# Merge stage by pairs of column chunks: another order of the branch products, and the gate tanh released earlier

## The chip, the cores and the metric

The kernel runs on one NeuronCore of one Trainium2 chip. The metric is the device time of one execution in microseconds. Before the change three runs took 836.33, 837.1 and 837.5 us, so the median is 837.1 us. The profile was taken from one more execution of 836.26 us.

## The reference, cut to what matters

One layer works on 512 tokens of width 1024. After an RMS norm, one projection makes the inputs of two branches, a matrix memory ("mLSTM", 4 heads of 128) and a differential attention (4 heads of 128), and two gates of width 1024. Each branch ends in a head norm. Then both branches go through a 512x1024 matrix of their own and are merged by the gates. An output projection, a gated feed-forward part, an embedding part and a last norm follow.

```
hm = head_rmsnorm(mlstm_chunkwise(...));  ya = (sigmoid(mo) * hm) @ w_br_m
hd = head_rmsnorm(diff_attention(...)) * (1 - lam_init);  yb = hd @ w_br_d
mixed = sigmoid(g_a) * ya + sigmoid(g_b) * yb
x = x + mixed @ w_out
```

## The kernel before

Activations lie with features on the 128 partitions and the 512 tokens along the free axis. So a vector of width 1024 is eight chunks of 128x512, and the result of one branch is four chunks, one per head (hm0 to hm3 of the memory, hd0 to hd3 of the attention). To keep precision every operand is split into a high and a low part (`split`, L86, recorded as L88 and L89, or L91 and L92 where there is a scale: ScalarE rounds to the high part, VectorE subtracts to get the low one). A product is then three matmuls, L96, L97 and L98 of `mm3`: high x high, low x high, high x low. In the products of the merge the weight is what the matmul calls whi and wlo.

Weights come by `wload` (L100): 512 KB from HBM into a buffer `raw`, then the split into `whi` and `wlo`. There are two buffers of each. The load and the split are given a raised priority, so they stand early in the order of their engines. A new `whi` can be written only when the last matmul that reads the old one in its buffer, an L97, has run.

The work of the two branches and of the first gates is written in the order of the table ORDER (L49). Its entries are steps such as `a3` (scores and probabilities of attention head 3), `A3` (the norm that ends that head) or `ga1` (a gate chunk), and a scheduler then sets the order of each engine at build time by priorities, data and free buffers. The last step is A3, that is `attention_end` (L491) for head 3: square (L405), a sum over the partitions on TensorE (`colsum`, tile hd3ss), VectorE L495, then `rsqrt_of` (L152: ScalarE Ln L157, Exp L159, Square L160, VectorE L161 and L162), VectorE L497 and the split that gives hdh and hdl of head 3.

The merge (L549 to L565) runs over eight column chunks j. For each it has two gate chunks (those for j = 0 to 3 come from the ORDER table, those for 4 to 7 are made in the loop), their tanh (L555, released by `issue_after` only when the last Exp of an `rsqrt_of` has been issued, which is that of head 3), one weight load that holds the 512 rows of the memory branch and the 512 of the attention branch for this column chunk, the products ya and yb of 12 matmuls each into two of the four PSUM buffers "mm", and on VectorE L560 to L562, which weight and add them, before the split into mxh and mxl. Two more PSUM buffers with the tag "acc" serve the two branches: num and den of the memory, av of the attention. ScalarE's activation functions come in table sets; a change of set is an instruction of its own, ACT_TABLE_LOAD.

Of the kernel before, what the change touches and what calls it, by code (L numbers as in the profile page):

```python
# [13 lines left out]
AF = mybir.ActivationFunctionType  # L14
ALU = mybir.AluOpType

P = 128
S = 512
D = 1024
KD = D // P  # L20
# [35 lines left out]
def trunk_kernel(ctx, tc, xT, pT, par, biasT, lamv, w_if, w_in, w_v, w_br, w_out, w_up,  # L56
                 w_down, w_gate, w_ple, gfin, out):
    nc = tc.nc
# [10 lines left out]
    def rt(tag, name):  # L69
        return big.tile([P, S], F32R, tag=tag, name=name, bufs=NBUF[tag])  # L70
# [5 lines left out]
    def ps(tag, name, n=S):  # L76
        return pp.tile([P, S], F32, tag=tag, name=name, bufs={"mm": 4, "sc": 2, "acc": 2}[tag])[:, :n]
# [8 lines left out]
    def split(hi, lo, src, scale=None):  # L86
        if scale is None:
            nc.scalar.copy(hi, src)  # L88
            nc.vector.tensor_sub(lo, src, f(hi))  # L89
        else:  # L90
            nc.scalar.activation(hi, src, AF.Copy, scale=scale)  # L91
            nc.vector.scalar_tensor_tensor(lo, src, scale, f(hi), op0=ALU.mult, op1=ALU.subtract)  # L92
# [7 lines left out]
    def wload(src, n=1024):  # L100
        raw = wp.tile([P, 1024], F32, tag="raw", name="raw", bufs=2)
        hi = wp.tile([P, 1024], F32R, tag="whi", name="whi", bufs=2)
        lo = wp.tile([P, 1024], F32R, tag="wlo", name="wlo", bufs=2)
        with tc.high_priority(offset=180):
            nc.sync.dma_start(raw[:, :n], src)
            split(hi[:, :n], lo[:, :n], raw[:, :n])
        return hi, lo
# [4 lines left out]
    def proj(o, w, k0, acts, start=True, stop=True):  # L112
        n = len(acts)
        for i, a in enumerate(acts):
            mm3(o, wk(w, k0 + i), a, start and i == 0, stop and i == n - 1)
# [14 lines left out]
    lnb = cp.tile([P, 1], F32, name="lnb")  # L130
# [16 lines left out]
            nc.scalar.activation(q, src, AF.Square)  # L147
            nc.vector.tensor_add(acc, acc, q)

    last_exp = None  # L150

    def rsqrt_of(r, v, a, before=None):  # L152

        if before is not None:
            with tc.issue_after(before.ins):
                nc.scalar.preload_act_table_set("natural_log_exp_and_others")
        nc.scalar.activation(r, v, AF.Ln, scale=2.0 ** -LN_SHIFT)  # L157
        nonlocal last_exp
        last_exp = nc.scalar.activation(r, r, AF.Exp, scale=-0.5, bias=lnb)  # L159
        nc.scalar.activation(a, r, AF.Square)  # L160
        nc.vector.scalar_tensor_tensor(a, v, -0.5, a, op0=ALU.mult, op1=ALU.mult)  # L161
        nc.vector.scalar_tensor_tensor(r, a, 1.5, r, op0=ALU.add, op1=ALU.mult)  # L162
# [19 lines left out]
    acc = tt("mo", "acc")  # L182
# [273 lines left out]
        return hi, lo  # L456


    def attention(hh, q, k):
        av = []  # L460
        for i in range(NB):
            n = (i + 1) * P
            nw = max(n, 2 * P)
            es, sums = [], []
            for z in range(2):
                s = ps("sc", f"ds{hh}{i}{z}", nw)
                for b in range(2):
                    nc.tensor.matmul(s, lhsT=q[z][:, i * P:(i + 1) * P], rhs=k[z][b][:, :nw],  # L468
                                     start=b == 0, stop=b == 1)
                e = tt("e" if z == 0 else "rb", f"e{z}", n)  # L470
                mx = tp.tile([P, 4], F32, tag="mx", name="mx", bufs=8)
                nc.vector.tensor_tensor_reduce(  # L472
                    out=e, in0=s[:, :n], in1=bias[hh][:, S - n:], scale=1.0, scalar=-3.0e38,
                    op0=ALU.add, op1=ALU.max, accum_out=mx[:, 0:1])
                nc.vector.tensor_scalar_mul(mx[:, 1:2], mx[:, 0:1], -1.0)  # L475
                nc.scalar.activation(e, e, AF.Exp, bias=mx[:, 1:2], accum_out=mx[:, 2:3])  # L476
                nc.vector.reciprocal(mx[:, 3:4], mx[:, 2:3])
                es.append(e)
                sums.append(mx[:, 3:4])
            nc.vector.tensor_scalar(es[1], es[1], sums[1], nlam, op0=ALU.mult, op1=ALU.mult)  # L480
            nc.vector.scalar_tensor_tensor(es[0], es[0], sums[0], es[1], op0=ALU.mult, op1=ALU.add)
            av.append(es[0])
        o = ps("acc", f"av{hh}")
        for j in range(NB):
            tps = ps("sc", f"at{hh}{j}", S - j * P)
            for i in range(j, NB):
                nc.tensor.transpose(tps[:, (i - j) * P:(i - j + 1) * P], av[i][:, j * P:(j + 1) * P], ident)
            weighted("a", j, lambda a, b: split(a, b, tps), dv, hh, (o,))
        return o
# [12 lines left out]
    def gate(c, name):  # L502
        o = ps("mm", name)
        proj(o, win(c), 0, h)
        t = tt("x", name)
        nc.vector.tensor_mul(t, o, rB)
        return t
# [3 lines left out]
    mq, mk, dq, dk, mo, sums, hm, hd, ga, gb = ({} for _ in range(10))  # L511
    for step in ORDER.split():
        what, i = step[:-1], int(step[-1])
# [18 lines left out]
        elif what == "bias":  # L532
            bias, nlam = make_bias(), make_nlam()
# [12 lines left out]
    hm, hd = ([t[i] for i in range(H)] for t in (hm, hd))  # L546


    mixed = []  # L549
    for j in range(KD):  # L550
        ta = ga[j] if j in ga else gate(20 + j, "ga")
        tb = gb[j] if j in gb else gate(28 + j, "gb")
        with tc.issue_after(last_exp.ins):
            for t in (ta, tb):
                nc.scalar.activation(t, t, AF.Tanh, scale=0.5)  # L555
        w = wload(w_br[j])
        oa, ob = ps("mm", "ya"), ps("mm", "yb")
        proj(oa, w, 0, hm)
        proj(ob, w, 4, hd)
        nc.vector.scalar_tensor_tensor(ta, ta, 1.0, oa, op0=ALU.add, op1=ALU.mult)  # L560
        nc.vector.scalar_tensor_tensor(tb, tb, 1.0, ob, op0=ALU.add, op1=ALU.mult)
        nc.vector.tensor_add(ta, ta, tb)  # L562
        hi, lo = rt("v", f"mxh{j}"), rt("v", f"mxl{j}")
        split(hi, lo, ta, 0.5)
        mixed.append((hi, lo))  # L565


    x2, h2 = [], []
    acc = tt("mo", "acc")
# [27 lines left out]
    for c in range(KF):  # L597
# [4 lines left out]
        hi, lo = rt(gtag[c], f"gh{c}"), rt(gtag[c], f"gl{c}")  # L602
# [10 lines left out]
    for k in range(2):  # L613
        t = tt("hn", "pt")
# [10 lines left out]
    for n in range(2):  # L625
        w = wload(w_ple[n])
# [10 lines left out]
    acc = tt("mo", "acc")  # L637
# [140 lines left out]
def _chunks(w):  # L778

    k, n = w.shape  # L780
    return w.reshape(k // P, P, n // P, P).transpose(2, 1, 0, 3).reshape(n // P, P, k)
# [25 lines left out]
def _pack(x, p, rel_bias, norm_mix_g, w_in, b_if, m_conv_w, m_conv_b, m_norm_g, da_lambda, da_norm_g,  # L807
          w_br_m, w_br_d, w_out, norm_ffn_g, w_up, ffn_conv_w, ffn_conv_b, w_down, norm_ple_g,
          w_ple_gate, w_ple, norm_final_g):
    w = w_in[0]  # L810
    mq, mk, mv, mo = (w[:, 512 * i:512 * (i + 1)] for i in range(4))
    gif = np.zeros((D, 64), np.float32)
    gif[:, 0:H] = w[:, 2048:2052]
    gif[:, 32:32 + H] = w[:, 2052:2056]
    dq, dk, dv = (w[:, 2056 + 512 * i:2056 + 512 * (i + 1)] for i in range(3))
    win = np.concatenate([mq, mk, dq, dk, mo, w[:, 3592:]], axis=1)
    wv = np.concatenate([v.reshape(4, 2, P, S).transpose(0, 2, 1, 3).reshape(4, P, 2 * S) for v in (mv, dv)])
    nf = DFF // P
    order = np.stack([nf + np.arange(nf), np.arange(nf)], axis=1).ravel()
    wup = _chunks(w_up[0])[order]  # L820
    par = np.zeros((P, NPAR), np.float32)
    for c, v in ((C_GMIX, norm_mix_g[0]), (C_GFFN, norm_ffn_g[0]), (C_GPLE, norm_ple_g[0]),
                 (C_GM, m_norm_g[0]), (C_GD, da_norm_g[0])):
        v = _cols(v)
        par[:, c:c + v.shape[1]] = v
    mc = np.concatenate([m_conv_w[0], m_conv_b], axis=0)
    par[:, C_MCONV:C_MCONV + 40] = mc.reshape(5, 8, P).transpose(2, 1, 0).reshape(P, 40)
    fc = np.concatenate([ffn_conv_w[0], ffn_conv_b], axis=0)
    par[:, C_FCONV:C_FCONV + 176] = fc.reshape(4, 2 * nf, P)[:, order].transpose(2, 1, 0).reshape(P, 176)
    par[0:H, C_B] = b_if[0, :H]  # L830
    par[32:32 + H, C_B] = b_if[0, H:]
    return {
        "xT": _fmajor(x[0]), "pT": _fmajor(p[0, 0]), "par": par, "biasT": _bias_tiles(rel_bias),
        "lamv": da_lambda[0],
        "w_if": gif.reshape(KD, P, 64).transpose(1, 0, 2).reshape(P, KD * 64), "w_in": _chunks(win), "w_v": wv,
        "w_br": np.concatenate([_chunks(w_br_m[0]), _chunks(w_br_d[0])], axis=2),
        "w_out": _chunks(w_out[0]), "w_up": wup, "w_down": _chunks(w_down[0]),
        "w_gate": w_ple_gate[0].reshape(KD, P, D), "w_ple": w_ple[0].reshape(2, P, 2, S).transpose(2, 1, 0, 3).reshape(2, P, D), "gfin": norm_final_g[None],
    }
# [18 lines left out]
```

## Time and profile before

| | |
|---|---|
| median of 3 runs | 837.1 us (836.33 to 837.5) |
| profiled execution | 836.26 us |
| its span, first to last instruction | 833.3 us |
| mean granted TensorE clock | 0.992 of full speed |
| TensorE matmuls | 811.2 us busy, 97% |
| VectorE / ScalarE | 539.7 us (65%) / 397.8 us (48%) |
| HBM | 101 GB/s over the span |

The page gives the busy time of each engine, the span in 40 slices with the granted clock, and the chain of work that ended last. A timeline row has the start in us, the duration, the engine, the line in the kernel, the operation, output and inputs by the program's names, shapes and a count; in brackets stands the idle time ahead of it and what ended it. A full-speed matmul of 512 columns is shown as 0.39 us long, but the next one starts 0.23 us later, because matmuls overlap.

### The profile page before, as it was taken

To read this page: it belongs to the slowest core of one execution; us is meant where nothing else is said; L and a number is where in the kernel's file an instruction comes from. 1 tells how busy PE (TensorE), PEld (TensorE's weight loads), DVE (VectorE), ACT (ScalarE), POOL (GpSimd) and SP (SyncE) were. 2 spreads that over 40 slices of the span, in tenths; PEclk is the share of its full clock that TensorE was granted. 3 is DMA by queue.
4 is the path that set the end of the run, shared out by engine and by line. 5 is a ranking of instruction groups with operands and counts; after the bars stand their busy time and mean duration, and the time that the engine had idled before them with its cause. 6 is when DMAs were issued, how large, how long until landed. Compare 5 with 4: busy or idle time off the path is not lost.

```text
span 833.3 us, 9859 instructions
## 1 busy us (share of the span) xinstructions
PE 811.2 (97%) x3661; PEld 665.4 (80%) x3661; DVE 539.7 (65%) x873; ACT 397.8 (48%) x614; POOL 27.3 (3%) x111
## 2 busy tenths in 40 slices
PE   8999999999999699999999999999999999999995
PEld 6878878878777588888788888888888888888884
DVE  7689885589977654455677777777777333343545
ACT  6546854487664632334554444444444432232434
POOL 0011200000000000000000000000000000000000
PEclk9999999999999899999999999999999999999998
DMA  6242532212222122252322222223223323333402
GB/s 245 77 131 98 174 115 74 101 51 76 77 77 76 51 101 101 96 187 97 126 102 94 87 97 101 101 102 115 89 99 102 95 89 96 95 112 96 147 31 76
DMA packets 28119, 84.54 MB, mean 101 GB/s; under 512 B 3316, under 2 KB 4992, under 8 KB 28072
## 3 DMA queue, kind: packets, MB, share of 16 engines
q1 hardware_dynamic: 27256, 81.96, 28.9%
q0 software_dynamic: 528, 1.70, 0.7%
q8 instruction: 28, 0.46, 0.2%
q10 hardware_dynamic: 288, 0.27, 0.1%
q14 instruction: 19, 0.16, 0.1%
HBM read 81.79 MB, written 2.13 MB: 101 GB/s over the span
## 4 chain that ended last, share of the span: by engine, by line
PE 81%; ACT 2%; issue 1%; DVE 1%; POOL 0%; POOLq 0%; DVEq 0%; ACTq 0%
PE uv L96 5%; PE wd L98 5%; PE wd L96 5%; PE uv L98 5%; PE uv L97 5%; PE wd L97 5%; PE ug L96 5%; PE ug L98 5%; PE ug L97 5%; PE ga L96 2%; PE ga L98 2%; PE ga L97 2%; PE gb L98 2%; PE gb L97 2%; PE gb L96 2%; PE wo L96 2%
## 5 line engine op out<-in xcount | busy, mean ns | idle before, releaser
L88 ACT CAST whi<-raw 128x1024 fp32r<-128x1024 f32 (+1 forms) x136 | 137.7, 1013 | 221.5 <-issue 72.5
L89 DVE TENSOR_TENSOR wlo<-raw,whi 128x1024 fp32r<-128x1024 f32 (+2 forms) x135 | 159.3, 1180 | 89.5 <-ACT whi L88 88.1
L97 PE MATMUL wd<-gl,whi 128*128 128x512 f32 x176 | 68.5, 389 | 0.0
L98 PE MATMUL wd<-gh,wlo 128*128 128x512 f32 x176 | 68.5, 389 | 0.0
L96 PE MATMUL wd<-gh,whi 128*128 128x512 f32 x176 | 68.5, 389 | 0.0
L592 DVE SCALAR_TENSOR_TENSOR y<-u,prm,y 128x512 f32<-128x512 f32 x88 | 65.6, 749 | 1.5
L88 ACT CAST gh<-y 128x512 fp32r<-128x512 f32 x22 | 13.7, 622 | 55.6 <-DVE y L601 55.6
L587 DVE TENSOR_TENSOR u<-uv,rffn 128x512 f32<-128x512 f32 x22 | 15.2, 692 | 38.1 <-PE uv L98 38.1
L97 PEld LDWEIGHTS wd<-gl,whi 128*128 128x128 f32 x176 | 33.0, 188 | 6.9
L98 PEld LDWEIGHTS wd<-gh,wlo 128*128 128x128 f32 x176 | 33.0, 188 | 6.9
L96 PEld LDWEIGHTS wd<-gh,whi 128*128 128x128 f32 x176 | 33.0, 188 | 6.8
L590 ACT ACTIVATE y<-u,prm 128x512 f32<-128x512 f32 x44 | 35.7, 812 | 0.5 <-DVE u L587 0.3
L599 ACT ACTIVATE y<-y 128x512 f32<-128x512 f32 x22 | 13.9, 632 | 38.7 <-DVE y L592 38.7
L96 PE MATMUL wo<-mxh,whi 128*128 128x512 f32 x64 | 24.9, 389 | 0.0
L97 PE MATMUL wo<-mxl,whi 128*128 128x512 f32 x64 | 24.9, 389 | 0.0
L98 PE MATMUL wo<-mxh,wlo 128*128 128x512 f32 x64 | 24.9, 389 | 0.0
L89 DVE TENSOR_TENSOR gl<-y,gh 128x512 fp32r<-128x512 f32 x22 | 15.2, 692 | 14.7 <-ACT gh L88 14.7
L476 ACT ACTIVATE e<-e,mx 128x128 f32<-128x128 f32 (+3 forms) x32 | 17.8, 556 | 7.8 <-DVE mx L475 7.8
L96 PE MATMUL yb<-hdh,whi 128*128 128x512 f32 x32 | 13.2, 412 | 6.5 <-ACT hdh L91 6.5
L224 DVE SCALAR_TENSOR_TENSOR y<-u,prm,y 128x512 f32<-128x512 f32 x24 | 17.9, 744 | 0.1
L472 DVE CUSTOM_DVE_ANT_0 e<-ds,bias 128x128 f32<-128x128 f32 (+3 forms) x32 | 15.3, 484 | 3.2 <-PE ds L468 3.0
L575 DVE TENSOR_TENSOR x<-x,wo 128x512 f32<-128x512 f32 x8 | 5.5, 688 | 17.2 <-PE wo L98 17.2
(1081 smaller groups left out, 2200.8 us busy)
## 6 DMA issues: line engine op xcount, KB each, us to landing
raw<-in_w_up SPq DMA_DIRECT2D x44, 512.0 KB, 3.2
raw<-in_w_in SPq DMA_DIRECT2D x36, 512.0 KB, 3.2
raw<-in_w_down SPq DMA_DIRECT2D x16, 512.0 KB, 3.5
x<-in_xT SPq DMA_DIRECT2D x16, 256.0 KB, 4.7
raw<-in_w_br SPq DMA_DIRECT2D x8, 512.0 KB, 3.1
raw<-in_w_out SPq DMA_DIRECT2D x8, 512.0 KB, 3.3
raw<-in_w_gate SPq DMA_DIRECT2D x8, 512.0 KB, 3.3
raw<-in_w_down SPq DMA_DIRECT2D x8, 384.0 KB, 3.1
```

The costliest lines, as they stand in the source:

```text
L88: nc.scalar.copy(hi, src)
L89: nc.vector.tensor_sub(lo, src, f(hi))
L96: nc.tensor.matmul(o, lhsT=lh, rhs=rh, start=start, stop=False)
L97: nc.tensor.matmul(o, lhsT=lh, rhs=rl, start=False, stop=False)
L98: nc.tensor.matmul(o, lhsT=ll, rhs=rh, start=False, stop=stop)
L224: nc.vector.scalar_tensor_tensor(y, u[:, i:i + S], col(c0 + i), y, op0=ALU.mult, op1=ALU.add)
L472: nc.vector.tensor_tensor_reduce(out=e, in0=s[:, :n], in1=bias[hh][:, S - n:], scale=1.0, scalar=-3.0e38, op0=ALU.add, op1=ALU.max, accum_ ...
L476: nc.scalar.activation(e, e, AF.Exp, bias=mx[:, 1:2], accum_out=mx[:, 2:3])
L587: nc.vector.tensor_mul(u[:, 2:514], o, rB)
L590: nc.scalar.activation(y, u[:, 2:514], AF.Identity, scale=col(c0 + 2), bias=col(c0 + 3))
L592: nc.vector.scalar_tensor_tensor(y, u[:, i:i + S], col(c0 + i), y, op0=ALU.mult, op1=ALU.add)
L599: nc.scalar.activation(gt, gt, AF.Gelu_apprx_tanh)
```

## The change

The merge loop now runs over pairs of column chunks (m = 0, 2, 4, 6). The weight array is laid out anew on the host: a load of 512 KB holds one branch for both chunks of the pair, the first the memory branch's, the second the attention branch's. So the order of the products in a pair is ya, ya, yb, yb, with a weight load ahead of each two. The two ya of the second pair (m = 2) take their PSUM from the tag "acc". The tanh of the gates is released by the last Exp of a softmax in `attention` in place of the last Exp of an `rsqrt_of`. The arithmetic is the same.

```diff
--- before.py
+++ after.py
@@ -147,16 +147,13 @@
             nc.scalar.activation(q, src, AF.Square)
             nc.vector.tensor_add(acc, acc, q)
 
-    last_exp = None
-
     def rsqrt_of(r, v, a, before=None):
 
         if before is not None:
             with tc.issue_after(before.ins):
                 nc.scalar.preload_act_table_set("natural_log_exp_and_others")
         nc.scalar.activation(r, v, AF.Ln, scale=2.0 ** -LN_SHIFT)
-        nonlocal last_exp
-        last_exp = nc.scalar.activation(r, r, AF.Exp, scale=-0.5, bias=lnb)
+        nc.scalar.activation(r, r, AF.Exp, scale=-0.5, bias=lnb)
         nc.scalar.activation(a, r, AF.Square)
         nc.vector.scalar_tensor_tensor(a, v, -0.5, a, op0=ALU.mult, op1=ALU.mult)
         nc.vector.scalar_tensor_tensor(r, a, 1.5, r, op0=ALU.add, op1=ALU.mult)
@@ -456,7 +453,10 @@
         return hi, lo
 
 
+    last_softmax = None
+
     def attention(hh, q, k):
+        nonlocal last_softmax
         av = []
         for i in range(NB):
             n = (i + 1) * P
@@ -473,7 +473,7 @@
                     out=e, in0=s[:, :n], in1=bias[hh][:, S - n:], scale=1.0, scalar=-3.0e38,
                     op0=ALU.add, op1=ALU.max, accum_out=mx[:, 0:1])
                 nc.vector.tensor_scalar_mul(mx[:, 1:2], mx[:, 0:1], -1.0)
-                nc.scalar.activation(e, e, AF.Exp, bias=mx[:, 1:2], accum_out=mx[:, 2:3])
+                last_softmax = nc.scalar.activation(e, e, AF.Exp, bias=mx[:, 1:2], accum_out=mx[:, 2:3])
                 nc.vector.reciprocal(mx[:, 3:4], mx[:, 2:3])
                 es.append(e)
                 sums.append(mx[:, 3:4])
@@ -546,23 +546,28 @@
     hm, hd = ([t[i] for i in range(H)] for t in (hm, hd))
 
 
+
     mixed = []
-    for j in range(KD):
-        ta = ga[j] if j in ga else gate(20 + j, "ga")
-        tb = gb[j] if j in gb else gate(28 + j, "gb")
-        with tc.issue_after(last_exp.ins):
-            for t in (ta, tb):
+    for m in range(0, KD, 2):
+        js = (m, m + 1)
+        gates = [(ga[j] if j in ga else gate(20 + j, "ga"), gb[j] if j in gb else gate(28 + j, "gb")) for j in js]
+        with tc.issue_after(last_softmax.ins):
+            for t in (t for pr in gates for t in pr):
                 nc.scalar.activation(t, t, AF.Tanh, scale=0.5)
-        w = wload(w_br[j])
-        oa, ob = ps("mm", "ya"), ps("mm", "yb")
-        proj(oa, w, 0, hm)
-        proj(ob, w, 4, hd)
-        nc.vector.scalar_tensor_tensor(ta, ta, 1.0, oa, op0=ALU.add, op1=ALU.mult)
-        nc.vector.scalar_tensor_tensor(tb, tb, 1.0, ob, op0=ALU.add, op1=ALU.mult)
-        nc.vector.tensor_add(ta, ta, tb)
-        hi, lo = rt("v", f"mxh{j}"), rt("v", f"mxl{j}")
-        split(hi, lo, ta, 0.5)
-        mixed.append((hi, lo))
+        outs = []
+        for n, (tag, ys) in enumerate((("acc" if m == 2 else "mm", hm), ("mm", hd))):
+            w = wload(w_br[m + n])
+            outs.append([ps(tag, ("ya", "yb")[n]) for _ in js])
+            for i in range(2):
+                proj(outs[n][i], w, 4 * i, ys)
+        for i, j in enumerate(js):
+            ta, tb = gates[i]
+            nc.vector.scalar_tensor_tensor(ta, ta, 1.0, outs[0][i], op0=ALU.add, op1=ALU.mult)
+            nc.vector.scalar_tensor_tensor(tb, tb, 1.0, outs[1][i], op0=ALU.add, op1=ALU.mult)
+            nc.vector.tensor_add(ta, ta, tb)
+            hi, lo = rt("v", f"mxh{j}"), rt("v", f"mxl{j}")
+            split(hi, lo, ta, 0.5)
+            mixed.append((hi, lo))
 
 
     x2, h2 = [], []
@@ -833,7 +838,8 @@
         "xT": _fmajor(x[0]), "pT": _fmajor(p[0, 0]), "par": par, "biasT": _bias_tiles(rel_bias),
         "lamv": da_lambda[0],
         "w_if": gif.reshape(KD, P, 64).transpose(1, 0, 2).reshape(P, KD * 64), "w_in": _chunks(win), "w_v": wv,
-        "w_br": np.concatenate([_chunks(w_br_m[0]), _chunks(w_br_d[0])], axis=2),
+        "w_br": np.stack([_chunks(v[0]).reshape(4, 2, P, S).transpose(0, 2, 1, 3).reshape(4, P, 2 * S)
+                          for v in (w_br_m, w_br_d)], axis=1).reshape(KD, P, 2 * S),
         "w_out": _chunks(w_out[0]), "w_up": wup, "w_down": _chunks(w_down[0]),
         "w_gate": w_ple_gate[0].reshape(KD, P, D), "w_ple": w_ple[0].reshape(2, P, 2, S).transpose(2, 1, 0, 3).reshape(2, P, D), "gfin": norm_final_g[None],
     }
```

The order on ScalarE, from the split of the weights loaded last before the attention's end (aph: high part of the turned probabilities of head 3; av3: its output; whi: weights; ga, gb: gates). Before:

```order
L88 CAST whi_2742<-raw_2741 128x1024
L88 CAST aph_2504<-at30_2499 128x512
L88 CAST aph_2515<-at31_2511 128x384
L88 CAST aph_2525<-at32_2522 128x256
L88 CAST aph_2534<-at33_2532 128x128
L493 ACTIVATE y_2675<-av3_2498,prm_72 128x512
L405 ACTIVATE v_2676<-av3_2498 128x512
L166 CAST csph_2681<-v_2676 128x512
L157 ACTIVATE r_2677<-v_2676 128x512
L159 ACTIVATE r_2677<-r_2677,lnb_91 128x512
L555 ACT_TABLE_LOAD
L555 ACTIVATE ga_2293<-ga_2293 128x512
```

In the changed program, from the same place:

```order
L88 CAST whi_2735<-raw_2734 128x1024
L556 ACT_TABLE_LOAD
L556 ACTIVATE ga_2293<-ga_2293 128x512
L556 ACTIVATE gb_2640<-gb_2640 128x512
L556 ACTIVATE gb_2359<-gb_2359 128x512
L88 CAST aph_2504<-at30_2499 128x512
L88 CAST aph_2515<-at31_2511 128x384
L556 ACTIVATE ga_2673<-ga_2673 128x512
L556 ACTIVATE ga_2326<-ga_2326 128x512
L556 ACTIVATE gb_2607<-gb_2607 128x512
L556 ACTIVATE ga_2061<-ga_2061 128x512
L88 CAST aph_2525<-at32_2522 128x256
```

and farther on, from the next weight split to the end of head 3 (hdh3):

```order
L402 ACTIVATE v_2676<-av3_2498 128x512
L163 CAST csph_2681<-v_2676 128x512
L155 ACT_TABLE_LOAD
L155 ACTIVATE r_2677<-v_2676 128x512
L156 ACT_TABLE_LOAD
L156 ACTIVATE r_2677<-r_2677,lnb_91 128x512
L157 ACTIVATE hd3ss_2680<-r_2677 128x512
L88 CAST whi_2817<-raw_2816 128x1024
L91 ACTIVATE hdh3_2694<-y_2675 128x512
```

One table load and seven tanh now stand ahead of or between the four casts aph, and an eighth behind them. Ln and Exp of head 3 have a table load each, and a weight cast (whi_2817) stands ahead of hdh3.

The order on TensorE at the last matmuls ahead of those that read hdh3 (yb_2707 and yb_2748 are yb of column chunks 0 and 1, ya_2788 is ya of chunk 2). Before:

```order
L98 MATMUL yb_2748<-hdh1_1930,wlo_2743 128x512
L96 MATMUL yb_2748<-hdh2_2258,whi_2742 128x512
L97 MATMUL yb_2748<-hdl2_2259,whi_2742 128x512
L98 MATMUL yb_2748<-hdh2_2258,wlo_2743 128x512
L96 MATMUL yb_2707<-hdh3_2694,whi_2701 128x512
L97 MATMUL yb_2707<-hdl3_2695,whi_2701 128x512
L98 MATMUL yb_2707<-hdh3_2694,wlo_2702 128x512
L96 MATMUL yb_2748<-hdh3_2694,whi_2742 128x512
L97 MATMUL yb_2748<-hdl3_2695,whi_2742 128x512
L98 MATMUL yb_2748<-hdh3_2694,wlo_2743 128x512
L96 MATMUL ya_2788<-hmh0_1907,whi_2783 128x512
```

In the changed program (yb_2740 and yb_2741 are yb of chunks 0 and 1, ya_2791 is ya of chunk 3, yb_2822 and yb_2823 are yb of chunks 2 and 3):

```order
L97 MATMUL ya_2791<-hml3_2415,whi_2785 128x512
L98 MATMUL ya_2791<-hmh3_2414,wlo_2786 128x512
L96 MATMUL yb_2822<-hdh0_1770,whi_2817 128x512
L97 MATMUL yb_2822<-hdl0_1771,whi_2817 128x512
L96 MATMUL yb_2823<-hdh0_1770,whi_2817 128x512
L96 MATMUL yb_2740<-hdh3_2694,whi_2735 128x512
L96 MATMUL yb_2741<-hdh3_2694,whi_2735 128x512
L97 MATMUL yb_2823<-hdl0_1771,whi_2817 128x512
L98 MATMUL yb_2822<-hdh0_1770,wlo_2818 128x512
L96 MATMUL yb_2822<-hdh1_1930,whi_2817 128x512
L97 MATMUL yb_2822<-hdl1_1931,whi_2817 128x512
L97 MATMUL yb_2740<-hdl3_2695,whi_2735 128x512
```

Between the last yb on hdh2 of chunk 1 and the first matmul on hdh3 stand now the 24 matmuls of ya of chunks 2 and 3 (ya_2790 and ya_2791, of which the piece shows the last two rows) and three matmuls on the weights whi_2817, which are split into the buffer that ya_2791's weights held.

## Rows read from the trace of the kernel before

**Rows 1.** The page, busy time, share of the span and instructions of each engine:
```profile
PE 811.2 (97%) x3661; PEld 665.4 (80%) x3661; DVE 539.7 (65%) x873; ACT 397.8 (48%) x614; POOL 27.3 (3%) x111
```

**Rows 2.** Waits of TensorE: us in total, times, longest:
```profile
PE yb L96 <- ACT hdh L91: 6.5, 1, 6.5
...
PE s L96 <- ACT mk0h L91: 1.4, 1, 1.4
```

**Rows 3.** Timeline of TensorE, from the wait to the gates behind the fourth chunk:
```profile
273.81 0.39 PE L98 MATMUL yb<-hdh,wlo 128*128 128x512 f32 x1
280.68 0.79 PE L96 MATMUL yb<-hdh,whi 128*128 128x512 f32 x1 [6.48 <-ACT hdh L91]
...
284.84 0.40 PE L98 MATMUL ya<-hmh,wlo 128*128 128x512 f32 x1
...
295.08 0.39 PE L96 MATMUL ga<-h0h,whi 128*128 128x512 f32 x1
...
300.07 0.39 PE L97 MATMUL ga<-h7l,whi 128*128 128x512 f32 x1
...
300.52 0.39 PE L96 MATMUL gb<-h0h,whi 128*128 128x512 f32 x1
```

**Rows 4.** Stretches: us, busy time by engine, granted clock (PEclk), DMA share, GB/s:
```profile
60.00:62.00 2.00, 0.66 (x3) 0.49 (x3) 1.30 (x2) 1.62 (x3) 1.02 (x3) 1.00 0.53 178
...
277.00:278.00 1.00, 0.00 (x0) 0.00 (x0) 0.97 (x3) 1.00 (x3) 0.00 (x0) 0.92 0.00 0
278.00:279.00 1.00, 0.00 (x0) 0.00 (x0) 1.00 (x2) 1.00 (x4) 0.00 (x0) 0.50 0.00 0
...
284.00:285.00 1.00, 1.00 (x4) 0.73 (x4) 1.00 (x2) 0.56 (x1) 0.00 (x0) 0.67 0.00 0
...
295.00:327.70 32.70, 32.70 (x146) 27.07 (x145) 15.28 (x18) 9.69 (x12) 0.00 (x0) 1.00 0.28 97
```

**Rows 5.** Timeline of ScalarE, from the last softmax on:
```profile
260.64 1.05 ACT L88 CAST whi<-raw 128x1024 fp32r<-128x1024 f32 x1
264.41 0.97 ACT L88 CAST aph<-at 128x512 fp32r<-128x512 f32 x2 [2.72 <-PE at L487]
267.37 0.54 ACT L88 CAST aph<-at 128x256 fp32r<-128x256 f32 x2 [1.99 <-PE at L487]
...
270.48 0.62 ACT L166 CAST csph<-v 128x512 fp32r<-128x512 f32 x1
273.14 0.63 ACT L157 ACTIVATE r<-v 128x512 f32<-128x512 f32 x1 [2.04 <-DVE v L495]
273.80 0.72 ACT L159 ACTIVATE r<-r,lnb 128x512 f32<-128x512 f32 x1
274.54 1.28 ACT L555 ACT_TABLE_LOAD   x1
275.84 0.63 ACT L555 ACTIVATE ga<-ga 128x512 f32<-128x512 f32 x1
...
280.01 0.61 ACT L91 ACTIVATE hdh<-y 128x512 fp32r<-128x512 f32 x1
...
300.54 1.05 ACT L88 CAST whi<-raw 128x1024 fp32r<-128x1024 f32 x1 [3.18 <-PE ga L97]
...
408.20 1.28 ACT L156 ACT_TABLE_LOAD   x1
```

**Rows 6.** Timeline of VectorE, in the norm of head 3 and in the gates:
```profile
277.10 0.69 DVE L161 SCALAR_TENSOR_TENSOR hd3ss<-v,hd3ss 128x512 f32<-128x512 f32 x1
...
301.62 1.23 DVE L89 TENSOR_TENSOR wlo<-raw,whi 128x1024 fp32r<-128x1024 f32 x1 [0.21 <-ACT whi L88]
```

**Rows 7.** Timeline of TensorE, attention output and square sum of head 3:
```profile
265.05 0.50 PE L96 MATMUL av<-aph,dvh 128*128 128x512 f32 x1
...
271.95 0.42 PE L169 MATMUL hd3ss<-cspl,ones 128*128 128x512 f32 x1
```

**Rows 8.** Timeline of SP's DMA queue: the four weight loads of chunks 0 to 3:
```profile
242.80 20.51 SPq L105 DMA_DIRECT2D raw<-in_w_br  x4
```

## The prediction

> **What bounds the kernel now.** I read the busy line of the page first: TensorE is busy for 97% of the span, no other engine for over 80% [rows 1]. So a gain must come from time in which TensorE stands still or runs at less than full speed. The list of TensorE's waits gives one large one: 6.5 us, before a yb, on ScalarE's cast to hdh; the next are 1.4 us [rows 2]. The timeline puts it at 274 to 281 us, where the attention's last head ends and the merge cannot go on without it [rows 3]. The stretches of 1 us then show that the wait costs more than its length: the granted clock is 0.92 at 277 us and 0.50 from 278 us, that is the lower level of 1.2 GHz, after TensorE had been idle since 274, and in 284 to 285, with TensorE back at work since 280.7, it is 0.67 on its way back [rows 4].
>
> The price of the stall: full-speed matmuls of 512 columns start 5.44 us apart per 24 (295.08 to 300.52), that is 0.227 each [rows 3]. The last start ahead of the wait is 273.81, the next 280.68: 6.87 less 0.23 is 6.64 us without work. From 280.68 to 284.84 nine matmuls start in 4.16 us instead of 2.04: 2.12 us at the lower clock [rows 3]. Together 8.76 us.
>
> Behind the stall, in the rest of the merge, TensorE is busy for all of 32.70 us at full clock with DMA at 28% [rows 4]. No other limit waits there to take back a gain.
>
> **The change, part by part.**
>
> *More work ahead of head 3.* Before, the merge stopped after two column chunks, since the third needs a weight buffer that the matmuls on hdh3 still hold. By pairs, the memory branch's weights are done with early and their buffer takes those of ya for chunks 2 and 3, whose products go to the attention's PSUM. The order shows 24 more matmuls ahead of the first on hdh3: 24 x 0.227 = 5.44 us of work moved into the stall, which then begins at 274.04 + 5.44 = 279.48. The number of matmuls stays the same, so what counts is only how long TensorE stands still now. ScalarE reads av3 for the last time before its csph cast at 270.48 [rows 5], ahead of the first of these 24 at 274.04, so this PSUM is free in time. The four weight loads were issued from 242.80 to 263.31 [rows 8], so the data is there.
>
> *What ends the new stall.* The next rows in the order read whi_2817, which goes into the buffer that the 24 matmuls have just read. Such a cast starts 0.47 after the start of the last L97 (300.07 to 300.54) and takes 1.05 [rows 3, 5]; TensorE follows ScalarE by 0.06 (280.01 + 0.61 to 280.68) [rows 3, 5]. From the L97's start that is 1.58 us, of which two slots (0.45) hold work: 1.13 us lost, from 279.48 to 280.61.
>
> *Is head 3 there by then?* I follow the chain from the rows of before. Three more matmuls stand ahead of the second hd3ss matmul, so 271.95 [rows 7] becomes 272.63 and Ln moves from 273.14 [rows 5] to 273.82. The table load ahead of Ln waits for nothing and runs behind the csph cast, as the one at 408.20 does [rows 5]: hidden. The load ahead of Exp is on the chain. Ln to Exp is 0.66, the load 1.28 [rows 5]: Exp at 275.8, Square at 276.5, and L161's successor could start at 277.1. In VectorE's queue a product with ya_2790 stands ahead of it, which waits for TensorE until about 277.0 and takes 0.69, so it starts at 277.7. Three VectorE instructions of 0.69 at most [rows 6] end by 279.8. So y is ready 0.7 ahead of ScalarE, which is casting whi_2817 from 279.5 to 280.55; hdh3 follows and ends at 281.1. Three matmuls on whi_2817 (280.61 to 281.29) cover it. wlo_2818 takes 1.23 [rows 6] from 280.6, to 281.85; its first matmul is the seventh, at 281.97. hdl3 ends 0.6 later, its first reader is the tenth, at 282.65. All fit, with 0.1 to 0.2 us to spare. I add 0.1 for one that does not: 1.2 us lost.
>
> *The clock there.* TensorE waited 1.42 us in 60 to 62 us and the granted clock stayed at 1.00 [rows 2, 4]. So I take no loss of clock for 1.2 us. If it fell for as long as before it would cost 2.12: that end I keep.
>
> *The tanh moved.* Eight tanh start 0.52 apart (from the first at 275.84 to hdh at 280.01 are eight steps, six more tanh and a Square between them [rows 5]), with one table load of 1.28. Before, a load and seven of them lay on the chain of head 3. Now the load and three go into the idle 2.72 ahead of the first aph: from the end of the weight cast at 260.64 + 1.05 = 261.69 they end at 264.55, against 264.41 before [rows 5]. Four, 2.08 long, go into the idle 1.99 ahead of the third aph [rows 5]. So av3 is late by at most 0.25, and TensorE has one more matmul (0.23) ahead of the first av, which started at 265.05 [rows 7]: nothing is left but a tenth or two. If none of it were covered it would cost all 2.84 + 2.08 = 4.9 us.
>
> *Table loads.* The Trainium skill, ScalarE: Activation LUTs, section on what ACT_TABLE_LOAD costs, puts a change of set at 2.66 us, of which 1.28 is the load and the rest a drain. It also wants calls batched by set, and this change adds a change back and forth. This case's trace has the load at 1.28 us and the tanh behind it 1.30 after its start (the load ends at 275.82, the tanh row at 275.84), so no drain is seen there. By the page, 1.38 would be added ahead of aph and again on the chain of head 3; the sum would be some 2 us less, about 831.7 us.
>
> *Later pairs.* Four gates, then ya, ya, yb, yb, with one weight load per 24 matmuls as before; the matmuls on one load take 5.44 us, its cast and subtraction 1.05 and 1.23 [rows 5, 6]. These pairs cost and give nothing; that TensorE is busy without a gap in 295 to 327.7 [rows 4] is the cover.
>
> **Sum.** 8.76 less 1.2 is 7.56, less a tenth for the av casts: 7.5 us. The profiled execution of 836.26 (span 833.3) becomes 828.8, its span about 825.8. It stood 0.8 us below the median of the three runs, 837.1, so the median becomes 829.6; I say 829.6.
>
> **The rivals.**
>
> *The stall is shorter but not short* (0.16). Either the clock falls in it (2.1 us), or table changes cost more than their rows, or wlo, hdl and ya_2790 in VectorE's queue come late one behind the other. Rows against the first: 1.00 in 60 to 62. For the last: margins of only 0.1 to 0.2. Time: 829.6 + 2.1 = 831.7 us.
>
> *No stall at all* (0.03): if ScalarE's cast overlapped the last ya. It cannot, by the buffer, but if 1.13 is too much by my reading the time is 828.4 us.
>
> *The gain is not there* (0.04): the chain of head 3 becomes so much later that the 24 matmuls are eaten up. With the clock's loss the same stall as before needs hdh3 at 286.1 in place of 281.1. Against it stands that all the added work of ScalarE on the chain is one load of 1.28. Time: 836 to 837 us.
>
> *Slower* (0.05): ScalarE runs its queue in order, and tanh now stand ahead of the four aph casts. A tanh that waits for its gate product on VectorE holds aph, so av3 and all of head 3, and TensorE with it. If none of three table loads (3.84) and eight tanh (4.16) fell into idle time, TensorE would stand still for 8.0 us more beside the 1.2, with 2.1 at the lower clock: 8.0 + 1.2 + 2.1 - 8.76 = 2.5 us slower, 839.6 us. It decides from 7.5 us of added waits. For it: the engine's order. Against it: the idle 2.72 and 1.99 just there, and that the gate multiplies precede in VectorE's order.
>
> **How the numbers follow.** The forecast holds 0.72, with a range of its own from 828.6 to 830.6 (spread of three runs, 0.6 to either side, and half a microsecond for margins missed). 0.2% is 1.7 us, about what a measurement of this kernel can tell from no change. Faster: 0.72 + 0.16 + 0.03 = 0.91; same 0.04; slower 0.05. For 8 in 10 the range goes from 827.9 to 832.6: it takes in the second case and leaves out those of no gain and of a loss.
>
> **What would show it.** In the changed profile TensorE's longest wait should be about 1.1 us, before a yb and on ScalarE's cast of whi, at about 279.5, with the granted clock at 1.00 around it; the gates of the fifth chunk should start near 287.5 in place of 295.08. ScalarE should show the tanh at 262 to 268.5, ahead of or between the aph casts, and the two loads around Ln. It is wrong if av starts over 0.5 us later than 265.05, if the wait is on hdh and over 2 us, if the clock falls to 0.50, or if TensorE stands still anywhere in the later pairs.

## The result, and the profile after

The changed kernel took 828.44 us (median of 4 runs, 827.62 to 829.77) where the kernel before took 836.72 us (4 runs, 835.06 to 837.5). The ratio is 0.9905 with a 95% interval from 0.9883 to 0.9927, that is 6.1 to 9.8 us faster. Run twice more beside the experiments below, it came out at 0.9905 (0.989 to 0.992) and 0.9893 (0.988 to 0.9905). The forecast was 829.6 us, 7.5 us below the median before as it was then, 837.1 us.

The profiled execution took 827.77 us, with a span of 826.0 us (before 836.26 and 833.3). The two differences, 8.5 and 7.3 us, are not the same, since 2.96 us of the execution before lie outside its span and 1.77 us of this one. TensorE's waits in the profile after (total, times, longest in us) answer to [rows 2]:

```profile
PE s L96 <- ACT mk0h L91: 1.4, 1, 1.4
...
PE yb L96 <- ACT whi L88: 0.9, 1, 0.9
...
PE av L96 <- ACT aph L88: 0.2, 1, 0.2
```

The wait of 6.5 us on hdh is gone. In its place stands one of 0.9 us on a weight cast; the 1.4 us ahead of s and the 0.2 us ahead of av were there before. TensorE's timeline after at that place, which answers to [rows 3]:

```profile
274.20 0.39 PE L98 MATMUL yb<-hdh,wlo 128*128 128x512 f32 x1
...
279.42 0.39 PE L97 MATMUL ya<-hml,whi 128*128 128x512 f32 x1
279.64 0.39 PE L98 MATMUL ya<-hmh,wlo 128*128 128x512 f32 x1
280.94 0.50 PE L96 MATMUL yb<-hdh,whi 128*128 128x512 f32 x1 [0.91 <-ACT whi L88]
...
287.88 0.39 PE L96 MATMUL ga<-h0h,whi 128*128 128x512 f32 x1
```

The old stall began behind the first of these rows. Now 24 matmuls run from there to 279.64. Then 1.30 us pass to the next start, 1.07 more than the 0.23 of a slot. The stretches answer to [rows 4]; the clock is the column ahead of the DMA share:

```profile
279.00:280.00 1.00, 1.00 (x5) 0.53 (x3) 0.97 (x2) 0.16 (x1) 0.00 (x0) 1.00 0.00 0
280.00:281.00 1.00, 0.09 (x2) 0.06 (x1) 0.84 (x3) 1.00 (x2) 0.00 (x0) 1.00 0.00 0
281.00:282.00 1.00, 1.00 (x5) 0.82 (x6) 1.00 (x1) 0.42 (x1) 0.00 (x0) 1.00 0.00 0
...
287.00:319.70 32.70, 32.70 (x146) 27.09 (x145) 18.02 (x23) 10.84 (x15) 0.00 (x0) 1.00 0.31 109
```

The granted clock stays at its upper level, 2.4 GHz, through the short wait, and the rest of the merge has no gap, as before. ScalarE's timeline after answers to [rows 5]:

```profile
261.37 1.05 ACT L88 CAST whi<-raw 128x1024 fp32r<-128x1024 f32 x1
262.44 1.28 ACT L556 ACT_TABLE_LOAD   x1
263.74 0.63 ACT L556 ACTIVATE ga<-ga 128x512 f32<-128x512 f32 x1
...
265.31 0.95 ACT L88 CAST aph<-at 128x512 fp32r<-128x512 f32 x2
...
268.37 0.54 ACT L88 CAST aph<-at 128x256 fp32r<-128x256 f32 x2
...
272.13 1.28 ACT L155 ACT_TABLE_LOAD   x1
274.20 0.63 ACT L155 ACTIVATE r<-v 128x512 f32<-128x512 f32 x1 [0.79 <-DVE v L495]
274.85 1.28 ACT L156 ACT_TABLE_LOAD   x1
276.15 0.72 ACT L156 ACTIVATE r<-r,lnb 128x512 f32<-128x512 f32 x1
...
279.84 1.04 ACT L88 CAST whi<-raw 128x1024 fp32r<-128x1024 f32 x1 [2.34 <-PE ya L97]
280.80 0.63 ACT L91 ACTIVATE hdh<-y 128x512 fp32r<-128x512 f32 x1
```

The first of these rows is 0.73 us later than before (260.64 to 261.37), since the first ya of the merge already starts later. Before:

```profile
260.63 0.40 PE L96 MATMUL ya<-hmh,whi 128*128 128x512 f32 x1
```

and after:

```profile
261.36 0.39 PE L96 MATMUL ya<-hmh,whi 128*128 128x512 f32 x1
```

The program ahead of it is unchanged, and in the ten profiles of this study that part ends between 260.63 and 262.57. Stretches are therefore compared from the first ya of the merge to the first gate matmul of chunk 4. That takes 34.45 us before (260.63 to 295.08) and 26.52 after (261.36 to 287.88): 7.93 us less.

What was won there stays. The first matmul of the output projection, behind all eight chunks, in the profile before:

```profile
360.36 0.39 PE L96 MATMUL wo<-mxh,whi 128*128 128x512 f32 x1
```

and after:

```profile
353.16 0.39 PE L96 MATMUL wo<-mxh,whi 128*128 128x512 f32 x1
```

It is 7.20 us earlier, exactly as the gate matmul (295.08 to 287.88), so the later pairs cost and gave nothing.

### The profile page after: what moved, and what is told of

The parts are those of the page before. It is cut to its first block, busy times and chain, and to the rows that moved or that the text cites. A ratio compares the mean times of both kernels' runs of the same rounds, so it can differ in the third digit from the quotient of the medians.

```text
span 826.0 us, 9860 instructions
## 1 busy us (share of the span) xinstructions
PE 809.2 (98%) x3661; PEld 664.6 (80%) x3661; DVE 539.6 (65%) x873; ACT 400.0 (48%) x616; POOL 27.4 (3%) x111
## 4 chain that ended last, share of the span: by engine, by line
PE 82%; issue 1%; ACT 1%; DVE 1%; POOL 0%; POOLq 0%; DVEq 0%; ACTq 0%
PE wd L96 5%; PE uv L97 5%; PE wd L97 5%; PE uv L98 5%; PE uv L96 5%; PE wd L98 5%; PE ug L97 5%; PE ug L98 5%; PE ug L96 5%; PE ga L96 2%; PE ga L97 2%; PE ga L98 2%; PE gb L98 2%; PE gb L97 2%; PE gb L96 2%; PE wo L96 2%
## 5 line engine op out<-in xcount | busy, mean ns | idle before, releaser
L96 PE MATMUL wd<-gh,whi 128*128 128x512 f32 x176 | 68.5, 389 | 0.0
L97 PE MATMUL wd<-gl,whi 128*128 128x512 f32 x176 | 68.5, 389 | 0.0
L98 PE MATMUL wd<-gh,wlo 128*128 128x512 f32 x176 | 68.5, 389 | 0.0
L98 PEld LDWEIGHTS wd<-gh,wlo 128*128 128x128 f32 x176 | 33.0, 188 | 6.9
L96 PEld LDWEIGHTS wd<-gh,whi 128*128 128x128 f32 x176 | 33.0, 188 | 6.9
L97 PEld LDWEIGHTS wd<-gl,whi 128*128 128x128 f32 x176 | 33.0, 188 | 6.8
L96 PE MATMUL wo<-mxh,whi 128*128 128x512 f32 x64 | 24.9, 389 | 0.0
L97 PE MATMUL wo<-mxl,whi 128*128 128x512 f32 x64 | 24.9, 389 | 0.0
L98 PE MATMUL wo<-mxh,wlo 128*128 128x512 f32 x64 | 24.9, 389 | 0.0
L591 POOL MEMSET u<- 128x2 f32 x44 | 4.4, 100 | 361.4 <-DVE y L597 350.1
```

The costliest lines, as they stand in the source:

```text
L96: nc.tensor.matmul(o, lhsT=lh, rhs=rh, start=start, stop=False)
L97: nc.tensor.matmul(o, lhsT=lh, rhs=rl, start=False, stop=False)
L98: nc.tensor.matmul(o, lhsT=ll, rhs=rh, start=False, stop=stop)
```

## The experiments

Two theories stood at first. One: the gain is the old stall, filled with 24 matmuls, and the slow matmuls behind it. The other: the gain is that a table load and seven tanh left the chain of head 3. Later runs ask what the clock alone is worth, whether the borrowed PSUM is needed, and what sets the rest of 1.07 us. The table gives the device time, the ratio to the kernel before on the same chip, and from the profile the stretch named above.

| kernel | median us | ratio (95%) | first ya to gate of chunk 4, us | against before |
|---|---|---|---|---|
| before | 836.0 and 836.5 | 1 | 260.63 to 295.08: 34.45 | |
| the change | 828.4 | 0.9905 (0.9890 to 0.9920) | 261.63 to 288.18: 26.55 | -7.90 |
| the change, again | 827.59 | 0.9893 (0.9880 to 0.9905) | 261.10 to 287.66: 26.56 | -7.89 |
| pairs only | 828.83 | 0.9912 (0.9899 to 0.9926) | 262.57 to 289.83: 27.26 | -7.19 |
| tanh only | 834.86 | 0.9994 (0.9984 to 1.0004) | 260.82 to 294.52: 33.70 | -0.75 |
| fill only | 834.51 | 0.9980 (0.9971 to 0.9989) | 260.78 to 294.29: 33.51 | -0.94 |
| no borrowed PSUM | 828.0 | 0.9909 (0.9892 to 0.9926) | 261.16 to 287.66: 26.50 | -7.95 |
| one table load | 827.3 | 0.9893 (0.9877 to 0.9909) | 261.30 to 287.09: 25.79 | -8.66 |
| free buffer | 828.14 | 0.9898 (0.9882 to 0.9914) | 260.96 to 286.52: 25.56 | -8.89 |

The device times tell the kernels with pairs from the kernel before, but not from each other: their intervals are over 2 us wide. There only the stretch of one profile decides; it agreed to 0.04 us in the three profiles of the change. The kernel before has one profile; fill only, the same program up to the stall, agrees with it to 0.02 us from the first ya to the first matmul on hdh3 (20.05 and 20.07 us). Behind the stretch the ten profiles agree too: 65.27 or 65.28 us to the first matmul of the output projection, and 472.76 to 472.94 us from there to the end. So what a kernel wins lies in the stretch.

**The change itself.** 

> The changed kernel itself, as the mark for the other runs. Theory (the gain is the old stall of TensorE, filled with 24 matmuls, and the lower clock behind it that no longer comes): 7.5 to 8.3 us below the kernel before. Rival (part of it is the spread between runs): 6 us or less.

> The changed kernel again, as the mark for the three runs beside it: 0.9905 of the kernel before, within 0.002.

It came out as the first theory has it: 7.6 us (836.03 less 828.4) and 8.9 us (836.53 less 827.59) by the medians, 7.9 in the stretch. The second ratio, 0.9893, lies within 0.002 of 0.9905.

**Pairs only.** The tanh wait again for the last Exp of the norms:

```diff
-        with tc.issue_after(last_softmax.ins):
+        with tc.issue_after(last_exp.ins):
```

> Pairs, new weight layout and PSUM of the change, but the tanh released as before by the last Exp of the norms. Theory (what counts is the work moved into the stall): TensorE stands still some 1 to 2 us longer than in the change, since hdh3 comes behind six tanh and a table load, at a full clock; 5.7 to 7 us below before. Rival (the gain comes from taking a load and seven tanh off the chain of head 3): 2 us below before or less.

It kept 7.19 of the 7.9 us, more than expected; by device time it can't be told from the change. TensorE's and ScalarE's rows at the stall of this kernel:

```profile
281.33 0.39 PE L98 MATMUL ya<-hmh,wlo 128*128 128x512 f32 x1
282.88 0.50 PE L96 MATMUL yb<-hdh,whi 128*128 128x512 f32 x1 [1.16 <-ACT whi L88]
```

```profile
281.27 0.61 ACT L559 ACTIVATE gb<-gb 128x512 f32<-128x512 f32 x1
281.79 1.03 ACT L88 CAST whi<-raw 128x1024 fp32r<-128x1024 f32 x1
282.73 0.63 ACT L91 ACTIVATE hdh<-y 128x512 fp32r<-128x512 f32 x1
```

The stall is 1.32 us (1.55 less a slot) in place of 1.07, because a tanh in ScalarE's queue holds the cast up for a quarter of a microsecond. Six tanh ahead of hdh3 cost no more there, since they ran under the 24 matmuls. The other half microsecond lies ahead of the stall: from the first ya to the last matmul before the 24 it is 13.32 us (262.57 to 275.89) in place of 12.84 (261.36 to 274.20). There a start comes 0.31 to 0.38 us after the one before it, in place of 0.23, eight times in this kernel and four times in the change. Three in each kernel stand just behind the transposes of head 3 (tile at). The others, five here and one in the change, are av, hd3ss or the matmul right behind one of these. So the second theory falls as the main cause: with the work moved in front of it the chain was no longer what TensorE waited for. The tanh's release is still worth some 0.7 us in the stretch.

**Tanh only.** The kernel before with the other release:

```diff
-        with tc.issue_after(last_exp.ins):
+        with tc.issue_after(last_softmax.ins):
```

> The kernel before, only the tanh released by the last softmax Exp. Theory: hdh3 comes some 1.4 us earlier (one load of 1.28 stays on the chain, for Exp, and only the tanh leave it), the stall is about 5 us in place of 6.5, the clock still falls to 0.50; 1 to 2 us below before. Rival (the tanh are most of the gain): 5 us or more below before.

The wait is 5.6 us, and the clock falls as before. TensorE's rows and two stretches of this kernel:

```profile
273.81 0.39 PE L98 MATMUL yb<-hdh,wlo 128*128 128x512 f32 x1
279.78 0.80 PE L96 MATMUL yb<-hdh,whi 128*128 128x512 f32 x1 [5.58 <-ACT hdh L91]
...
284.09 0.60 PE L98 MATMUL ya<-hmh,wlo 128*128 128x512 f32 x1
284.51 0.41 PE L96 MATMUL ya<-hmh,whi 128*128 128x512 f32 x1
```

```profile
278.00:279.00 1.00, 0.00 (x0) 0.00 (x0) 0.97 (x2) 0.00 (x0) 0.00 (x0) 0.50 0.00 0
...
284.00:285.00 1.00, 1.00 (x5) 0.73 (x3) 1.00 (x2) 0.63 (x1) 0.00 (x0) 0.74 0.35 111
```

TensorE resumes 0.9 us earlier than before, but the clock is back only in 284 to 285 us, as in [rows 4]. So ten matmuls run slowly in place of nine: 4.73 us for 2.27, a loss of 2.46 in place of 2.12. The gain in the stretch is 0.75 us, less than the 1 to 2 expected, and in device time it can't be told from nothing. Pairs alone and tanh alone add up to the whole, 7.19 + 0.75 = 7.94, but that is chance, since the tanh won in different places. Here it is 0.19 us ahead of the stall and 0.90 in it, less 0.34 in slow matmuls; between pairs only and the change it is 0.48 ahead of the stall and 0.25 in it.

**Fill only.** The kernel before, with 24 matmuls in the stall whose result nobody reads:

```diff
         proj(ob, w, 4, hd)
+        if j == 1:
+            fill = ps("acc", "fill")
+            for i in range(24):
+                nc.tensor.matmul(fill, lhsT=ones, rhs=h[i % KD][0], start=i == 0, stop=i == 23)
```

> The kernel before with 24 more matmuls of 512 columns into an unused PSUM buffer, issued in the stall; their result is not read. Theory (2.1 us of the old price is the clock): TensorE waits about 1.2 us, the granted clock stays at 1.00, the wait for hdh ends when it did; 1.8 to 2.3 us below before. Rival (the slow matmuls behind the stall would have waited for the low part of head 3 and the next weights anyway): no change within 0.5 us.

The clock stayed at 1.00 throughout. TensorE's rows and one stretch of this kernel:

```profile
279.41 0.39 PE L563 MATMUL fill<-h7h,ones 128*128 128x512 f32 x1
280.85 0.73 PE L96 MATMUL yb<-hdh,whi 128*128 128x512 f32 x2 [1.05 <-ACT hdh L91]
281.58 0.50 PE L97 MATMUL yb<-hdl,whi 128*128 128x512 f32 x1
...
283.21 0.50 PE L96 MATMUL ya<-hmh,whi 128*128 128x512 f32 x1 [0.44 <-ACT whi L88]
```

```profile
280.00:281.00 1.00, 0.15 (x1) 0.15 (x2) 0.17 (x1) 1.00 (x3) 0.00 (x0) 1.00 0.00 0
```

Both theories were half right. With the clock up, the matmuls on hdh3 are done sooner, but the next weights cannot be cast before the L97 among them has run, and TensorE waits for that cast (0.44 us in the row). The order there is not quite that of before either: both L96 on hdh3 now come first, where before an L97 and an L98 stood between them. So the test does not hold everything but the clock still. Of the 2.12 us only 0.94 are won in the stretch; the device time (0.2%, 0.1 to 0.3%) says 0.9 to 2.4 us.

**No borrowed PSUM.**

```diff
-        for n, (tag, ys) in enumerate((("acc" if m == 2 else "mm", hm), ("mm", hd))):
+        for n, (tag, ys) in enumerate((("mm", hm), ("mm", hd))):
```

> The change, but ya of the second pair takes its PSUM from the four general buffers like the others. Theory (VectorE frees ya of the first pair early, and the order on TensorE is the same): no more than 0.3 us from the change, since only yb of chunk 3 now waits for VectorE's product with ya of chunk 3, which ends at about 280.8, while that yb starts at 281.5. Rival (the borrowed PSUM is what lets the 24 matmuls run ahead): 2 us or more slower than the change.

The order on TensorE is the same, the wait too, and the stretch is 26.50 us against 26.52 to 26.56. With the order as it stands here the borrowed PSUM is worth nothing. Its row at the stall:

```profile
280.73 0.50 PE L96 MATMUL yb<-hdh,whi 128*128 128x512 f32 x1 [0.91 <-ACT whi L88]
```

**What sets the last 1.07 us.** Two kernels take away the wait on the cast by different ways. One loads a table set with Ln and Exp ahead of head 3's norm:

```diff
-        rsqrt_of(r, v, ss, None if hh else last)
+        rsqrt_of(r, v, ss, last if hh in (0, 3) else None)
```

> The change, with one table set for Ln and Exp loaded ahead of head 3's norm, so that Exp has no load of its own; by that hdh3 comes ahead of the cast whi_2818 in ScalarE's order, and the seven matmuls on it come ahead of those on that weight. Theory (the remaining stall of 1.07 us is the cast into a buffer that was read until just before): the seven matmuls cover the cast, the wait of 0.9 us goes; about 1 us below the change, 827.3 where the change has 828.4. Rival (the cast is only the last of several waits that end together): a wait of like size takes its place, on hdl or wlo; within 0.3 us of the change.

The other leaves the chain and puts the weights of yb of chunks 2 and 3 elsewhere (wfree is a copy of wload that splits the two halves of `raw` into tiles of the tag "qk", free since the scores of head 3):

```diff
-            w = wload(w_br[m + n])
+            ws = [(wload(w_br[m + n]), 0)] * 2 if (m, n) != (2, 1) else [(t, 0) for t in wfree(w_br[m + n])]
...
-                proj(outs[n][i], w, 4 * i, ys)
+                proj(outs[n][i], ws[i][0], 0 if (m, n) == (2, 1) else 4 * i, ys)
```

> The change, with the weights of yb of chunks 2 and 3 split into four free tiles instead of the buffer that ya_2791 reads, so that the cast needs no matmul to end. The table loads and tanh stay on head 3's chain. Theory: no wait at all at that place, about 1 us below the change, 827.3 where the change has 828.4. Rival (head 3's chain ends no earlier than the cast did, so TensorE waits for hdh3 instead): within 0.3 us of the change.

TensorE's rows of the kernel with one table load, and ScalarE's:

```profile
279.35 0.39 PE L97 MATMUL ya<-hml,whi 128*128 128x512 f32 x1
279.57 0.68 PE L96 MATMUL yb<-hdh,whi 128*128 128x512 f32 x2
280.10 0.40 PE L98 MATMUL ya<-hmh,wlo 128*128 128x512 f32 x1
...
281.99 0.40 PE L97 MATMUL yb<-hdl,whi 128*128 128x512 f32 x1
282.41 0.50 PE L98 MATMUL yb<-hdh,wlo 128*128 128x512 f32 x1
```

```profile
278.84 0.63 ACT L91 ACTIVATE hdh<-y 128x512 fp32r<-128x512 f32 x1 [2.68 <-DVE y L497]
279.77 1.05 ACT L88 CAST whi<-raw 128x1024 fp32r<-128x1024 f32 x1 [0.30 <-PE ya L97]
```

and TensorE's rows of the kernel with the free buffer:

```profile
279.32 0.39 PE L98 MATMUL ya<-hmh,wlo 128*128 128x512 f32 x1
279.55 0.39 PE L96 MATMUL yb<-hdh,wq0h 128*128 128x512 f32 x1
...
281.16 0.73 PE L96 MATMUL yb<-hdh,whi 128*128 128x512 f32 x2
```

Neither has a wait of over 0.2 us left there. In the first, hdh3 is ready ahead of the cast, and seven matmuls, six on head 3 and the last ya, cover the cast; a gap of 0.2 us remains before wlo (281.99 to 282.41). In the second, TensorE goes on from ya to yb in a slot's time with the table loads still on the chain, so it was the buffer that set the 1.07 us, not the chain of head 3. The stretch is 0.7 and 1.0 us shorter than in the change. By device time neither can be told from it (0.9893 and 0.9898 against 0.9893 beside them), so these two are better by the profile only.

## Why the prediction was right

*The bound and the price of the stall.* Right: 8.76 us were lost, and nothing downstream took the gain back. What was wrong is how the price was split. "2.12 us at the lower clock" is what the starts show, but fill only won 0.94 of it in the stretch, because the next weights were late behind the same matmuls (in a slightly different order). For the sum this did no harm: the change took away the stall and its aftermath together. From the last matmul ahead of the old stall to the gate it takes 13.68 us (274.20 to 287.88) where before it took 21.27 (273.81 to 295.08), 7.59 less, and 8.76 less 1.2 was 7.56.

*More work ahead of head 3.* Right: the last of the 24 matmuls starts 5.44 us behind the last start ahead of them (274.20 to 279.64). That their products go to the attention's PSUM was not needed, as the kernel without borrowed PSUM shows.

*What ends the new stall.* Right in place and size: a cast of whi, 1.13 us forecast, 1.07 measured. The cast starts 0.42 after the L97 (279.42 to 279.84) where 0.47 was taken. Another 0.13 is lost just behind it (next point), which makes 1.20; so the tenth that was added for a margin missed was used.

*Head 3 in time.* Right. VectorE's rows after:

```profile
277.35 0.69 DVE L565 SCALAR_TENSOR_TENSOR ga<-ga,ya 128x512 f32<-128x512 f32 x1 [3.18 <-PE ya L98]
...
279.40 0.69 DVE L497 TENSOR_TENSOR y<-y,r 128x512 f32<-128x512 f32 x1
...
280.92 1.23 DVE L89 TENSOR_TENSOR wlo<-raw,whi 128x1024 fp32r<-128x1024 f32 x1 [0.16 <-ACT whi L88]
282.06 0.69 DVE L92 SCALAR_TENSOR_TENSOR hdl<-y,hdh 128x512 fp32r<-128x512 f32 x1
```

y is ready at 280.09, 0.7 us ahead of ScalarE's hdh at 280.80, as forecast. The product with ya of chunk 2 (277.35) stands ahead of the norm's steps and waits for TensorE, as forecast. From 280.94 to 287.88 the 30 matmuls take 6.94 us where 30 slots are 6.81: nothing there was late by more than 0.13.

*The tanh moved.* Mis-sized, with the wrong sign: "a tenth or two" of loss at the aph casts. From the first ya to the last matmul ahead of the old stall the change takes 12.84 us where before it took 13.18 (260.63 to 273.81), a gain of 0.34. The casts come as forecast: aph at 3.94 us from the weight cast (261.37 to 265.31) against 3.77 before. But the starts that come over 0.30 us behind the one before them are four in place of seven, 0.1 us each. Three stand behind the transposes in all of these kernels; the rest, at av and hd3ss, are four before, one in the change, five in pairs only and two in tanh only. The part takes 13.32 us in pairs only and 12.99 in tanh only (260.82 to 273.81), so the gain comes with the tanh and not with the pairs. The first av is not the place: it starts 0.64 or 0.65 us after its cast both before and after (264.41 to 265.05, 265.31 to 265.96). Why the later ones cost less, and which of the moved rows does it, was not tried. This term, forecast as a loss of 0.1 and measured as a gain of 0.34, is nearly all of the difference between 7.5 and 7.93.

*The test on av.* The text said it would be wrong if av started over 0.5 us later than 265.05. It did:

```profile
265.96 0.47 PE L96 MATMUL av<-aph,dvh 128*128 128x512 f32 x1
```

Of the 0.91 us, 0.73 lie ahead of the merge. A mark in absolute time was the wrong mark: it should have been 4.42 us from the first ya before (260.63 to 265.05) and is 4.60 after.

*Table loads.* The row was the better guide. After, the load at 274.85 ends at 276.13 and Exp starts at 276.15; the one at 262.44 ends at 263.72 and tanh starts at 263.74. The Trainium skill, ScalarE: Activation LUTs, section on what ACT_TABLE_LOAD costs, adds a drain that brings a change of set to 2.66 us. These two loads show none, neither between load and function nor ahead of the load (the cast at 261.37 ends at 262.42, the load starts at 262.44). The same page of the Trainium skill, section on table sets, advises to batch calls by set. That did not decide here: the change has nine table loads in place of seven and is faster, and with one load fewer on the chain the stretch was 0.7 us shorter, with another order on ScalarE and TensorE.

*The rivals.* None came. Slower needed 7.5 us of added waits; 1.07 us at yb is all there is, beside the 0.2 at av that was there before.

*The number.* The 828.44 us lie within 827.9 to 832.6, but 0.16 below the forecast's own range of 828.6 to 830.6, and they are what the rival "no stall at all" gave (828.4). So the time alone does not tell these two apart; the profile does, with a stall of 1.07 us. Two things put the forecast too high: the tanh, by 0.4 us, and the 837.1 us that it started from, since later runs of the kernel before have medians of 836.03 and 836.53.

## What to carry to other kernels

Where the busiest engine stands still behind a serial chain, give it independent work first, and ask which buffer holds that work back; shortening the chain by itself won a tenth as much here (0.75 against 7.19 us in the stretch). Whether a third weight buffer in the old loop would do as much was not tried. Take a reorder's new wait from the order that the program will have: the next wait was a weight cast into a buffer read until just before, and its size could be summed from three rows. Do not count the slow matmuls behind a stall as a price of their own before asking what they would wait for at full clock.

## What the runs showed of the hardware

The clock came back within the same microsecond whether TensorE resumed at 280.68 (before: 0.67 in 284 to 285 us) or at 279.78 (tanh only: 0.74 there), so an earlier end of the stall bought slow matmuls with part of what it won. It did not fall in the wait of 1.4 us in 60 to 62 us [rows 2, 4], nor in pairs only, which waited 1.16 us (granted clock 1.00 from 280 to 284 us). A change of table set cost 1.30 us from the start of the load to the start of the function behind it (262.44 to 263.74 and 274.85 to 276.15).
